# The first four pairs of input tiles of the recurrent stage as seven products, with the residual reloaded behind them

## The chip, the core and the metric

The kernel runs on one core of a Trainium2 chip. The metric is the device time of one execution in microseconds (us); a time is the median of several executions. The trace comes from one execution under the hardware profiler.

## The reference

One decoder layer on 512 tokens of width 1024: a SwiGLU feed-forward, a mixing layer, a second feed-forward, each with an RMS norm in front and behind. The mixing layer, in which the change lies, is

```
u = rms_norm(h, mix_norm_pre)
q, k, v, xr, yr, gl = split(u @ w_in)          # 12 heads of q, k, v; xr, yr: 1024 wide; gl: 2048
attn = dilated_window_attention(q, k, v)        # three groups of heads, joined by their log-sum-exp
xc  = conv4(xr) + conv_b                        # causal, width 4, per channel
gate_x, gate_a = sigmoid(xc_head @ w_x + b_x), sigmoid(xc_head @ w_a + b_a)
log_a = -8 * gate_a * softplus(-a_param);  a = exp(log_a)
rec = scan(a, sqrt(1 - a*a) * gate_x * xc) * gelu(yr)
gates = sigmoid(gl)                             # two of width 1024
merged = gates[0] * (attn @ w_attn) + gates[1] * (rec @ w_rec)
h = h + rms_norm(merged @ w_out, mix_norm_post)
```

## The kernel before, in words

**Precision.** Every float32 operand is split in two float32r parts, hi and lo, by a copy on ACT and a subtraction on DVE (`split`, lines 284 and 285). A product is three matmuls: hi by hi, hi by lo, lo by hi (`mm3`, lines 297 to 299).

**Plain products.** The 512 tokens lie along the free axis. A tile of 128 output columns is `gemm`: 8 blocks of the 1024 inputs by three matmuls of 512 tokens, 24 in all, into one PSUM bank (`acc`, five of them; `aux`, three).

**Seven products.** Most of the feed-forwards and the q, k and first gate columns go another way. Two output tiles (called g and u) by two halves of the tokens by two halves of the input are a 2 x 2 by 2 x 2 block product, done with seven products in place of eight (Strassen and Winograd). Each of the seven is 4 blocks by three matmuls of 256 tokens, 12 matmuls (`seventh`, lines 616 to 618), so a pair of tiles takes 84 matmuls of 256 tokens in place of 48 of 512. It needs forms of both operands: sums of their quarters, split again. The forms of the mixing layer's input `u` are made once, in the attention stage (`forms_of`): p1, p2, p3 are its own quarters in `um`'s tiles, p5 and p7 are in two tiles of the pool tagged "b" (named `big`), p6 and p4 in two slots `tx` of the attention pool. The forms of a pair's weights are made for each pair (`w_forms`): four additions of 128x512 and splits of 1024, 1024, 1024 and 512 columns, in three of the four `w8` slots and one of the two `w4` slots; they need a scratch `s12`. The seven products are put together either by `seven` (three copies out of PSUM by ACT and four sums by DVE) or by `seven_on` (used in the feed-forwards), where the later products are added in PSUM onto copies of the earlier ones: four copies by ACT (one bank to another, or to SBUF), and PE comes back to the copied bank one product later. `seven_on` holds four `acc` banks.

**Order in the mixing layer.** Values; four heads, each with the q and k pairs of the next; four pairs of gate tiles; the attention branch's output product (8 tiles, 96 matmuls); then the recurrent stage in the order of `LRU_ORDER`: conv 0, branch 0, branch 1, conv 1, gates 0, branch 2, conv 2, gates 1, gate1 1, and so on. `conv` makes two tiles of `xr` with a plain product each, copies them in time order (line 1269, a strided copy), runs the four taps on ACT and DVE (1270, 1272) and splits the result into `rec`. `branch` makes two tiles of `yr`, copies them out (1286); `gelus` applies the Gelu for two heads after branches 1 and 3 (1292). `gates` makes the two gates of a head from `rec` (1322), and `recur` does the recurrence (1333 to 1351), and overwrites `rec` with its output.

**Order of the engines.** The program is written in one order, and a planner gives each engine a fixed order of its own by rank. The rank is the place in the program, moved forward by `tc.high_priority(offset)`: weights are fetched and split at `state["ahead"]`, 100 in most of the kernel (AHEAD) and 300 in the recurrent stage (EVAC + AHEAD); emptying a PSUM bank has 200 (EVAC). `w_forms` has 100. An engine then works strictly in its order.

**DMAs.** Weights come in 1 MB pieces through SP's queue into two `raw` buffers, in the order of `stream_plan`. The residual `h` was stored to DRAM as `kept_m` and is reloaded through POOL's queue (four DMAs of 512 KB, line 1216) after the last gate pair, into two tiles of the pool "b", which has six: four hold `um`. It is read again in the boundary behind the out product (line 461).

Of the kernel before, what the change touches and what calls it, by code (L numbers as in the profile page):

```python
# [16 lines left out]
P = 128  # L17
T = 512
# [27 lines left out]

# [37 lines left out]
def part_blocks(a):  # L84

    return (FF_PARTS[a][1] - FF_PARTS[a][0]) // 2


def stream_plan():

    plan = []

    def down(n, a, half):
        for kk in range(part_blocks(a)):
            plan.append((("down", n, a, half, kk), 1024))

    def ffn(n):
        for ev in ffn_order(n):
            if ev[0] == "std":
                plan.append((("gate", n, ev[1]), 1024))  # L100
                plan.append((("up", n, ev[1]), 1024))
            elif ev[0] == "prep":
                plan.append((("gu", n, ev[1]), 2048))
            elif ev[0] == "down":
                down(n, *ev[1:])
            elif ev[0] == "prepd":
                for q in SEVEN_RAW[ev[2]]:
                    plan.append((("dq", n, ev[1], q), 1024))
        for half in range(2):
            down(n, len(FF_PARTS) - 1, half)  # L110

    def values(g):
        for k in range(4):
# [12 lines left out]
    for h in range(NH):  # L126
        qk(h)
    for c in range(0, KC, 2):
        plan.append((("pair", 52 + c, 53 + c), 2048))
    for m in range(KC):  # L130
        plan.append((("attn", m), 512))
    for what, h in LRU_ORDER:
        if what == "gates":
            plan.append((("lru", h), 1024))
        else:
            cs = GATE1[h] if what == "gate1" else (2 * h, 2 * h + 1)
            o = {"conv": 36, "branch": 44, "gate1": 60}[what]
            for c in cs:
                plan.append((("in", o + c), 1024))
    for m in range(KC):  # L140
        plan.append((("rec", m), 1024))
    for half in range(2):
        for kk in range(4):
            plan.append((("out", half, kk), 1024))
    ffn(2)
    return plan
# [25 lines left out]
def hybrid_layer(ctx: ExitStack, tc: tile.TileContext, xT: bass.AP, xN: bass.AP, wst: bass.AP,  # L172
# [365 lines left out]
    def tx_slot(pool, bufs=1):  # L538
        return pool.tile([P, 2, 4, HB], F32R, name="tx", tag="tx", bufs=bufs)

    def forms_of(x, his, los, pool, copied):


        spool[0] = pool
        fx = facc.rearrange("p k t -> p (k t)").rearrange("p (b c) -> p b c", b=4)

        def quarter(i, j):
            return fx[:, 2 * j:2 * j + 2, i * T:i * T + T]

        def slot():  # L550
            return tx_slot(pool, 1 if copied else 2).rearrange("p s k t -> p s (k t)").rearrange(
                "p s (b c) -> p s b c", b=2)
# [36 lines left out]
    spool = [None]  # L589

    def w_forms(key):

        with tc.high_priority(offset=AHEAD):
            raw = raw_of(key)
            u0, u1, g0, g1 = (raw[:, i * 512:(i + 1) * 512] for i in range(4))
            s12 = spool[0].tile([P, 2, 512], F32, name="s12", tag="s", bufs=2)
            DVE.tensor_add(s12[:, 1, :], u0, u1)  # L597
            DVE.tensor_add(s12[:, 0, :], s12[:, 1, :], g0)
            DVE.tensor_add(u0, u0, g0)
# [17 lines left out]
            PE.matmul(ps, wh, xl, start=False, stop=False, skip_group_check=True)  # L617
            PE.matmul(ps, wl, xh, start=False, stop=k == 3, skip_group_check=True)  # L618

    def seven_on(t, w, g, u):  # L620

        b, z, y, v = (acc_ps()[:, :HB] for _ in range(4))
        lo, hi = HALVES

        def copy(ps, dst=None):
            if dst is None:
# [2 lines left out]
                ACT.activation(dst, ps, AF.Copy)  # L631
            return dst

        def sum_of(dst, ps, c):
            with tc.high_priority(offset=EVAC):
                DVE.tensor_add(dst, ps, c)

        seventh(t, w, "p1", b, True)
        copy(b, y)
        seventh(t, w, "p5", z, True)  # L640
# [1 line left out]
        seventh(t, w, "p6", b, False)  # L642
        c6 = copy(b)
        seventh(t, w, "p2", y, False)
        ACT.activation(g[:, lo], y, AF.Silu)
        seventh(t, w, "p7", b, False)
        copy(b, v)
        sum_of(u[:, hi], b, c5)
        seventh(t, w, "p3", z, False)
        sum_of(g[:, hi], z, c6)  # L650
        ACT.activation(g[:, hi], g[:, hi], AF.Silu)
        seventh(t, w, "p4", v, False)
        return v

    def seven(t, w, z, g, u, seen=lambda ap: ap):

# [32 lines left out]
    def ffn(n, x, r, forms_x, apool, pss):  # L689
# [101 lines left out]
        def prod(f, w):  # L791
            g, u = tmp("g"), tmp("u")
            if f >= FIRST_ON[n]:
                v = seven_on(t, w, g, u)

                def put(dst, view):
                    for q, (h, src) in enumerate(zip(HALVES, (v, u[:, HALVES[1]]))):
                        DVE.scalar_tensor_tensor(dst[:, q] if len(dst.shape) == 3 else dst[:, h], g[:, h], -1.0, src,
                                                 op0=ALU.mult, op1=ALU.mult)
                into(f, put)  # L800
# [192 lines left out]
    ff1.close()  # L993


    with ExitStack() as mx:
        tpl = mx.enter_context(tc.tile_pool(name="attn_out", bufs=1))
        apool_cm = tc.tile_pool(name="attention", bufs=1)
# [51 lines left out]
        t, steps = forms_of(um, um_t[:2], um_t[2:], apool, False)  # L1050
        values(VALUES[0], True)
        attn_t = tpl.tile([P, 8, T], F32R, name="attn", tag="attn")
        attn = Act([attn_t[:, i, :] for i in range(4)], [attn_t[:, 4 + i, :] for i in range(4)])
# [157 lines left out]
            ACT.activation(facc[:, c, :], g, AF.Sigmoid)  # L1211
            ACT.activation(facc[:, c + 1, :], u, AF.Sigmoid, scale=-1.0)
        apool_cm.__exit__(None, None, None)
        new_h()
        for b in range(4):
            nc.gpsimd.dma_start(hb(b), kept_m[b])
        for c in range(KC):
            ps = acc_ps()
            gemm(ps, fetch(("attn", c)), attn)
# [1 line left out]

    with ExitStack() as mx:
        rpool = mx.enter_context(tc.tile_pool(name="rec", bufs=1))
        rec_t = rpool.tile([P, 16, T], F32R, name="rec")
        rec = Act([rec_t[:, i, :] for i in range(8)], [rec_t[:, 8 + i, :] for i in range(8)])
        sig = rpool.tile([P, KC, T], F32, name="sig")
        lpool_cm = tc.tile_pool(name="lru", bufs=1)
        lpool = lpool_cm.__enter__()

# [27 lines left out]
        def pi(ap):  # L1257
            return ap.rearrange("q (p i) -> q p i", p=4)

        def conv(hd):  # L1260

            for c in (2 * hd, 2 * hd + 1):
                ps = acc_ps()
                gemm(ps, fetch(("in", 36 + c)), um)
                xr = lpool.tile([P, 3 + T], F32, name="xr", tag="xr", bufs=2)
                DVE.memset(xr[:, 0:3], 0.0)
                xc = sig[:, c, :]
                with tc.high_priority(offset=EVAC):
                    DVE.tensor_copy(ip(xr[:, 3:]), pi(ps))
                    ACT.activation(xc, xr[:, 3:], AF.Identity, bias=col("cb", c), scale=col("cw", 3 * 8 + c))  # L1270
                    for t in (2, 1, 0):
                        DVE.scalar_tensor_tensor(xc, xr[:, t:t + T], col("cw", t * 8 + c), xc,
                                                 op0=ALU.mult, op1=ALU.add)
                    split(rec.hi[c], rec.lo[c], xc)
# [3 lines left out]
        def branch(hd):  # L1278

            gels[hd] = []  # L1280
            for c in (2 * hd, 2 * hd + 1):
                ps = acc_ps()
                gemm(ps, fetch(("in", 44 + c)), um)
# [67 lines left out]
                DVE.tensor_mul(pi(ge), ip(th), pi(ge))  # L1351
                split(rec.hi[c], rec.lo[c], ge)

        state["ahead"] = EVAC + AHEAD
        for what, hd in LRU_ORDER:
            if what == "gates":
                recur(hd, gels.pop(hd), *gates_of(hd))
            else:
# [13 lines left out]
        for c in range(KC):  # L1372
# [5 lines left out]
            DVE.tensor_mul(sig[:, c, :], ps, sig[:, c, :])  # L1378
            DVE.tensor_add(sig[:, c, :], sig[:, c, :], facc[:, c, :])
            split(mg.hi[c], mg.lo[c], sig[:, c, :])  # L1380


    ap2 = ctx.enter_context(tc.tile_pool(name="act2", bufs=1))
# [141 lines left out]
```

## Time and profile before

| | |
|---|---|
| median of 3 runs | 1227.24 us (1226.72 to 1227.56) |
| the profiled execution | 1227.1 us |
| its span in the trace | 1225.3 us |
| granted TensorE clock | 0.999 |
| the four pairs conv 0, branch 0, branch 1, conv 1 | 636.74 to 680.26 us of the span |
| the recurrent stage to the last gate | to about 800 us |

PE is TensorE's matmuls, PEld its weight loads, DVE VectorE, ACT ScalarE, POOL GpSimd, SP the queue that issues the weight DMAs. A row of a timeline has the start, the duration, engine, line, operation, output and inputs, and in brackets the idle time before it. The end of a matmul is modelled and overlaps the next, so its price is the distance between starts. A row of a group has the count, the busy time, the mean duration in ns, the idle time before and what ended it. The residual's reload stands at 611 to 614 us.

### The profile page before, as it was taken

What the parts mean: (1) busy time and instruction counts of PE and PEld (TensorE: products, weight loads), DVE (VectorE), ACT (ScalarE), POOL (GpSimd) and SP (SyncE); (2) the same over time, 40 slices, a digit from 0 to 9 for tenths busy, and PEclk for the clock granted to TensorE, in tenths of its full rate; (3) what the DMA queues carried; (4) which work ended last, traced back from release to release, by engine and by line L of the source; (5) the groups of instructions that cost most, each with busy time, mean ns of one, the idle gap of its engine ahead of it and who ended that gap; (6) DMA issues with size and microseconds to landing.
All of it is one profiled execution on the core that took longest, in us unless ns stands there. A gap on an engine that the chain in (4) does not pass through costs nothing.

```text
span 1225.3 us, 19182 instructions
## 1 busy us (share of the span) xinstructions
PE 1214.1 (99%) x7700; PEld 1102.8 (90%) x7700; DVE 981.5 (80%) x1497; ACT 784.0 (64%) x1337; POOL 26.1 (2%) x51
## 2 busy tenths in 40 slices
PE   9999999999999999999999999999999999999997
PEld 8899999999878899999988888888899999999996
DVE  7988888899677587888565897785798888889975
ACT  7556777777555365665543888844566677878752
POOL 0000000000002000000000000000100000000000
PEclk9999999999999999999999999999999999999999
DMA  6223333334614222222252222234453333333341
GB/s 246 89 84 121 121 121 121 121 121 167 245 69 146 89 93 103 79 78 103 73 204 74 98 104 74 98 110 168 151 156 121 121 120 121 121 120 121 138 172 69
DMA packets 29401, 148.73 MB, mean 121 GB/s; under 512 B 3200, under 2 KB 6400, under 8 KB 15232
## 3 DMA queue, kind: packets, MB, share of 16 engines
q1 hardware_dynamic: 22032, 130.20, 29.4%
q0 software_dynamic: 7280, 17.30, 4.1%
q8 instruction: 60, 0.98, 0.3%
q14 instruction: 29, 0.24, 0.1%
HBM read 137.01 MB, written 6.29 MB: 117 GB/s over the span
## 4 chain that ended last, share of the span: by engine, by line
PE 93%; DVE 3%; ACT 2%; DMA 1%; issue 0%; DVEq 0%; ACTq 0%
PE acc L616 14%; PE acc L617 14%; PE acc L618 14%; PE acc L297 8%; PE acc L298 8%; PE acc L299 8%; PE aux L879 3%; PE aux L880 3%; PE aux L881 3%; PE acc L403 2%; PE acc L405 2%; PE acc L404 2%; PE acc L1025 1%; PE acc L1027 1%; PE acc L1026 1%; DMA raw<-in_w 1%
## 5 line engine op out<-in xcount | busy, mean ns | idle before, releaser
L285 DVE TENSOR_TENSOR w<-raw,w 128x1024 fp32r<-128x1024 f32 (+1 forms) x274 | 296.3, 1086 | 75.8 <-ACT w L284 68.8
L616 PE MATMUL acc<-big,w 128*128 128x256 f32 x1208 | 342.8, 284 | 0.4 <-ACT c L631 0.4
L617 PE MATMUL acc<-big,w 128*128 128x256 f32 x1208 | 342.7, 284 | 0.0
L618 PE MATMUL acc<-big,w 128*128 128x256 f32 x1208 | 342.4, 283 | 0.0
L284 ACT ACTIVATE w<-raw 128x1024 fp32r<-128x1024 f32 (+1 forms) x274 | 258.5, 949 | 120.1 <-PE acc L299 36.7
L616 PEld LDWEIGHTS acc<-big,w 128*128 128x128 f32 x1208 | 231.5, 192 | 2.4 <-ACT c L631 1.0
L617 PEld LDWEIGHTS acc<-big,w 128*128 128x128 f32 x1208 | 231.6, 192 | 1.4
L618 PEld LDWEIGHTS acc<-big,w 128*128 128x128 f32 x1208 | 231.6, 192 | 0.0
L616 PE MATMUL acc<-tx,w 128*128 128x256 f32 x276 | 78.5, 284 | 0.0
L617 PE MATMUL acc<-tx,w 128*128 128x256 f32 x276 | 78.1, 283 | 0.0
L618 PE MATMUL acc<-tx,w 128*128 128x256 f32 x276 | 78.1, 283 | 0.0
L879 PE MATMUL aux<-w,xf 128*128 128x512 f32 x196 | 76.4, 393 | 0.8 <-ACT w L284 0.8
L880 PE MATMUL aux<-w,xf 128*128 128x512 f32 x196 | 76.6, 391 | 0.0
L881 PE MATMUL aux<-w,xf 128*128 128x512 f32 x196 | 76.3, 389 | 0.0
L297 PE MATMUL acc<-big,w 128*128 128x512 f32 x192 | 74.7, 389 | 0.0
L298 PE MATMUL acc<-big,w 128*128 128x512 f32 x192 | 74.7, 389 | 0.0
L299 PE MATMUL acc<-big,w 128*128 128x512 f32 x192 | 74.7, 389 | 0.0
L284 ACT ACTIVATE w<-s 128x1024 fp32r<-128x1024 f32 x53 | 56.0, 1058 | 19.7 <-PE acc L618 13.9
L285 DVE TENSOR_TENSOR w<-s,w 128x1024 fp32r<-128x1024 f32 x53 | 64.6, 1218 | 4.2 <-ACT w L284 4.2
L597 DVE TENSOR_TENSOR s<-raw 128x512 f32<-128x512 f32 x53 | 36.4, 687 | 32.7 <-DMA raw<-in_w 32.7
L616 PEld LDWEIGHTS acc<-tx,w 128*128 128x128 f32 x276 | 52.9, 192 | 0.1
L617 PEld LDWEIGHTS acc<-tx,w 128*128 128x128 f32 x276 | 52.9, 192 | 0.0
(367 smaller groups left out, 2572.2 us busy)
## 6 DMA issues: line engine op xcount, KB each, us to landing
raw<-in_w SPq DMA_DIRECT2D x110, 1024.0 KB, 4.8
raw<-in_w SPq DMA_DIRECT2D x14, 512.0 KB, 3.6
big<-xf POOLq DMA_DIRECT2D x6, 512.0 KB, 3.2
gains<-in_rows POOLq DMA_DIRECT2D x5, 512.0 KB, 4.9
h<-in_x SPq DMA_DIRECT2D x8, 256.0 KB, 5.1
h<-in_xn POOLq DMA_DIRECT2D x4, 512.0 KB, 5.6
kept_m<-h POOLq DMA_DIRECT2D x4, 512.0 KB, 2.9
h<-kept_m POOLq DMA_DIRECT2D x4, 512.0 KB, 5.2
```

The lines of the kernel that those rows point to most:

```text
L284: ACT.activation(dh, src, AF.Copy)
L285: DVE.tensor_sub(dl, src, dh.bitcast(F32))
L297: PE.matmul(ps, wh, xh, start=first, stop=False)
L298: PE.matmul(ps, wh, xl, start=False, stop=False)
L299: PE.matmul(ps, wl, xh, start=False, stop=last)
L597: DVE.tensor_add(s12[:, 1, :], u0, u1)
L616: PE.matmul(ps, wh, xh, start=start and k == 0, stop=False, skip_group_check=True)
L617: PE.matmul(ps, wh, xl, start=False, stop=False, skip_group_check=True)
L618: PE.matmul(ps, wl, xh, start=False, stop=k == 3, skip_group_check=True)
L879: PE.matmul(ps, xh, wh, start=first and j == 0, stop=False, skip_group_check=True)
L880: PE.matmul(ps, xh, wl, start=False, stop=False, skip_group_check=True)
L881: PE.matmul(ps, xl, wh, start=False, stop=j == 1, skip_group_check=True)
```

## The change

The first four input pairs of `LRU_ORDER` (conv 0, branch 0, branch 1, conv 1) are made with `seven_on` from the forms of the input that the attention stage made. The weights are streamed in pairs (the same bytes, in the same 1 MB pieces). `seven_on` takes functions for the four places where a half tile is finished; in the feed-forwards they do what they did, here they are four half-width DVE instructions at 200. The forms of the first pair are prepared in front of the stage at 100, those of the next at the start of each pair at 300, with `s12` in a free part of `sig`. The forms p6 and p4 now lie in one tile `rb` of a pool `keep` that stays open to the end of the stage; the second half of `rec` takes the same tile once the four pairs are done. The residual is reloaded there too, since p5 and p7 hold its two tiles until then.

```diff
+PAIRED = LRU_ORDER[:4]
+COLUMN = {"conv": 36, "branch": 44, "gate1": 60}
...
+        elif (what, h) in PAIRED:
+            plan.append((pair_key(what, h), 2048))
...
         def slot():
-            return tx_slot(pool, 1 if copied else 2).rearrange(
+            if not copied and not two:
+                v = rb()
+                two.extend(v[:, 4 * i:4 * i + 4, :].rearrange("p (s j) t -> p s j t", s=2) for i in range(2))
+            if two:
+                return two.pop(0)
+            return tx_slot(pool).rearrange("p s k t -> p s (k t)").rearrange("p s (b c) -> p s b c", b=2)
...
-    def w_forms(key):
+    def w_forms(key, s12=None):
-        with tc.high_priority(offset=AHEAD):
+        with tc.high_priority(offset=state["ahead"]):
...
-            s12 = spool[0].tile([P, 2, 512], F32, name="s12", tag="s", bufs=2)
+            if s12 is None:
+                s12 = spool[0].tile([P, 2, 512], F32, name="s12", tag="s", bufs=2)
...
-    def seven_on(t, w, g, u):
+    def seven_on(t, w, g0, g1, u0, u1):
...
         seventh(t, w, "p2", y, False)
-        ACT.activation(g[:, lo], y, AF.Silu)
+        g0(y)
         seventh(t, w, "p7", b, False)
         copy(b, v)
-        sum_of(u[:, hi], b, c5)
+        u1(b, c5)
         seventh(t, w, "p3", z, False)
-        sum_of(g[:, hi], z, c6)
-        ACT.activation(g[:, hi], g[:, hi], AF.Silu)
+        g1(z, c6)
         seventh(t, w, "p4", v, False)
-        return v
+        u0(v)
...
+    kpool_cm = tc.tile_pool(name="keep", bufs=1)
+    kpool = kpool_cm.__enter__()
+
+    def rec_half():
+        return kpool.tile([P, 8, T], F32R, name="rb", tag="rb")
...
         apool_cm.__exit__(None, None, None)
-        new_h()
-        for b in range(4):
-            nc.gpsimd.dma_start(hb(b), kept_m[b])
...
+        def prepare(i):
+            paired[PAIRED[i]] = w_forms(pair_key(*PAIRED[i]), sig[:, 4 + i % 2 * 2:6 + i % 2 * 2, :])
+
+        def pair_next(key):
+            if PAIRED.index(key) + 1 < len(PAIRED):
+                prepare(PAIRED.index(key) + 1)
+            return paired.pop(key)
+
+        prepare(0)
+        state["ahead"] = EVAC + AHEAD
...
+        def pairs_to(w, g, u, view, half):
+            def up(dst, ps, sign):
+                with tc.high_priority(offset=EVAC):
+                    if sign > 0:
+                        DVE.tensor_copy(half(dst, 0), view(ps))
+                    else:
+                        DVE.tensor_scalar(half(dst, 0), view(ps), -1.0, None, op0=ALU.mult)
+            def low(dst, ps, c, sign):
+                with tc.high_priority(offset=EVAC):
+                    if sign > 0:
+                        DVE.tensor_add(half(dst, 1), view(ps), view(c))
+                    else:
+                        DVE.scalar_tensor_tensor(half(dst, 1), view(ps), -1.0, view(c), op0=ALU.mult, op1=ALU.subtract)
+            seven_on(t, w, lambda y: up(g, y, 1), lambda z, c: low(g, z, c, 1), lambda v: up(u, v, -1),
+                     lambda b, c: low(u, b, c, -1))
...
         def conv(hd):
...
+            if ("conv", hd) in PAIRED:
+                w = pair_next(("conv", hd))
+                pairs_to(w, *(xr_of(2 * hd + i) for i in range(2)), lambda ap: ap.rearrange("q (p i) -> q p i", p=2),
+                         lambda x, i: x[:, 2 * i:2 * i + 2, :])
...
         def branch(hd):
...
+            if ("branch", hd) in PAIRED:
+                w = pair_next(("branch", hd))
+                gels[hd] = [lpool.tile([P, T], F32, name="ge", tag="ge", bufs=6) for _ in range(2)]
+                pairs_to(w, *gels[hd], lambda ap: ap, lambda x, i: x[:, HALVES[i]])
+                return
...
         for what, hd in LRU_ORDER:
+            if len(paired) == 0 and rec.hi[4:] == [] and (what, hd) not in PAIRED:
+                rec_t = rec_half()
+                rec.hi += [rec_t[:, i, :] for i in range(4)]
+                rec.lo += [rec_t[:, 4 + i, :] for i in range(4)]
+                new_h()
+                for b in range(4):
+                    nc.gpsimd.dma_start(hb(b), kept_m[b])
```

More of the change, by code (lines that the diff above doesn't have):

```diff
@@ L86, in part_blocks, with pair_key @@
     return (FF_PARTS[a][1] - FF_PARTS[a][0]) // 2
+def pair_key(what, h):
+    c = COLUMN[what] + 2 * h
+    return "pair", c, c + 1
 def stream_plan():
@@ L134, in stream_plan @@
             plan.append((("lru", h), 1024))
-        else:
[L136 to L139, printed above, removed]
+        elif (what, h) in PAIRED:
+            plan.append((pair_key(what, h), 2048))
+        else:
+            for c in GATE1[h] if what == "gate1" else (2 * h, 2 * h + 1):
+                plan.append((("in", COLUMN[what] + c), 1024))
     for m in range(KC):
@@ L539, in tx_slot, with forms_of @@
         return pool.tile([P, 2, 4, HB], F32R, name="tx", tag="tx", bufs=bufs)
-    def forms_of(x, his, los, pool, copied):
+    def forms_of(x, his, los, pool, copied, rb=None):
         spool[0] = pool
@@ L548, in quarter @@
             return fx[:, 2 * j:2 * j + 2, i * T:i * T + T]
+        two = []
         def slot():
-            return tx_slot(pool, 1 if copied else 2).rearrange("p s k t -> p s (k t)").rearrange(
-                "p s (b c) -> p s b c", b=2)
+            if not copied and not two:
[4 more added lines that the diff above has]
+            return tx_slot(pool).rearrange("p s k t -> p s (k t)").rearrange("p s (b c) -> p s b c", b=2)
         x01, x10, x11 = quarter(0, 1), quarter(1, 0), quarter(1, 1)
@@ L618, in seventh @@
             PE.matmul(ps, wl, xh, start=False, stop=k == 3, skip_group_check=True)
-    def seven_on(t, w, g, u):
+    def seven_on(t, w, g0, g1, u0, u1):
         b, z, y, v = (acc_ps()[:, :HB] for _ in range(4))
-        lo, hi = HALVES
         def copy(ps, dst=None):
@@ L632, in copy @@
             return dst
-        def sum_of(dst, ps, c):
-            with tc.high_priority(offset=EVAC):
-                DVE.tensor_add(dst, ps, c)
         seventh(t, w, "p1", b, True)
@@ L793, in prod, with g1, u1, u0 @@
             if f >= FIRST_ON[n]:
[L794 to L800, printed above, removed]
+                lo, hi = HALVES
+                def g1(z, c6):
+                    with tc.high_priority(offset=EVAC):
+                        DVE.tensor_add(g[:, hi], z, c6)
+                    ACT.activation(g[:, hi], g[:, hi], AF.Silu)
+                def u1(b, c5):
+                    with tc.high_priority(offset=EVAC):
+                        DVE.tensor_add(u[:, hi], b, c5)
+                def u0(v):
+                    def put(dst, view):
+                        for q, (h, src) in enumerate(zip(HALVES, (v, u[:, hi]))):
+                            DVE.scalar_tensor_tensor(dst[:, q] if len(dst.shape) == 3 else dst[:, h], g[:, h], -1.0,
+                                                     src, op0=ALU.mult, op1=ALU.mult)
+                    into(f, put)
+                seven_on(t, w, lambda y: ACT.activation(g[:, lo], y, AF.Silu), g1, u0, u1)
                 return
@@ L1048, in values @@
                 vals[g] = nv
-        t, steps = forms_of(um, um_t[:2], um_t[2:], apool, False)
+        t, steps = forms_of(um, um_t[:2], um_t[2:], apool, False, rec_half)
         values(VALUES[0], True)
@@ L1223, in hybrid_layer @@
         rpool = mx.enter_context(tc.tile_pool(name="rec", bufs=1))
-        rec_t = rpool.tile([P, 16, T], F32R, name="rec")
-        rec = Act([rec_t[:, i, :] for i in range(8)], [rec_t[:, 8 + i, :] for i in range(8)])
+        rec_t = rpool.tile([P, 8, T], F32R, name="rec")
+        rec = Act([rec_t[:, i, :] for i in range(4)], [rec_t[:, 4 + i, :] for i in range(4)])
+        rec.n = KC
         sig = rpool.tile([P, KC, T], F32, name="sig")
+        paired = {}
+        def prepare(i):
[6 more added lines that the diff above has]
+        state["ahead"] = EVAC + AHEAD
         lpool_cm = tc.tile_pool(name="lru", bufs=1)
@@ L1258, in pi, with xr_of @@
             return ap.rearrange("q (p i) -> q p i", p=4)
-        def conv(hd):
-            for c in (2 * hd, 2 * hd + 1):
[L1263 to L1267, printed above, removed]
+        def pairs_to(w, g, u, view, half):
+            def up(dst, ps, sign):
+                with tc.high_priority(offset=EVAC):
+                    if sign > 0:
[3 more added lines that the diff above has]
+            def low(dst, ps, c, sign):
+                with tc.high_priority(offset=EVAC):
+                    if sign > 0:
[4 more added lines that the diff above has]
+                     lambda b, c: low(u, b, c, -1))
+        def conv(hd):
+            xrs = {}
+            def xr_of(c):
+                xrs[c] = lpool.tile([P, 3 + T], F32, name="xr", tag="xr", bufs=2)
+                DVE.memset(xrs[c][:, 0:3], 0.0)
+                return ip(xrs[c][:, 3:])
+            if ("conv", hd) in PAIRED:
+                w = pair_next(("conv", hd))
+                pairs_to(w, *(xr_of(2 * hd + i) for i in range(2)), lambda ap: ap.rearrange("q (p i) -> q p i", p=2),
+                         lambda x, i: x[:, 2 * i:2 * i + 2, :])
+            for c in (2 * hd, 2 * hd + 1):
+                if c not in xrs:
+                    ps = acc_ps()
+                    gemm(ps, fetch(("in", 36 + c)), um)
+                    with tc.high_priority(offset=EVAC):
+                        DVE.tensor_copy(xr_of(c), pi(ps))
+                xr, xc = xrs[c], sig[:, c, :]
                 with tc.high_priority(offset=EVAC):
-                    DVE.tensor_copy(ip(xr[:, 3:]), pi(ps))
                     ACT.activation(xc, xr[:, 3:], AF.Identity, bias=col("cb", c), scale=col("cw", 3 * 8 + c))
@@ L1352, in recur @@
                 split(rec.hi[c], rec.lo[c], ge)
-        state["ahead"] = EVAC + AHEAD
         for what, hd in LRU_ORDER:
+            if len(paired) == 0 and rec.hi[4:] == [] and (what, hd) not in PAIRED:
[5 more added lines that the diff above has]
+                    nc.gpsimd.dma_start(hb(b), kept_m[b])
             if what == "gates":
@@ L1380, in hybrid_layer @@
             split(mg.hi[c], mg.lo[c], sig[:, c, :])
+    kpool_cm.__exit__(None, None, None)
     ap2 = ctx.enter_context(tc.tile_pool(name="act2", bufs=1))
```

## The prediction, made before the result was known

> **What bounds the kernel now.** I read the busy times first, then the chain of work that ended last, then stretches of the stage that changes.
>
> ```profile
> span 1225.3 us, 19182 instructions
> PE 1214.1 (99%) x7700; PEld 1102.8 (90%) x7700; DVE 981.5 (80%) x1497; ACT 784.0 (64%) x1337; POOL 26.1 (2%) x51
> PE 93%; DVE 3%; ACT 2%; DMA 1%; issue 0%; DVEq 0%; ACTq 0%
> ```
>
> PE is busy 99% of the span and makes up 93% of the chain, so time can come only from fewer or shorter matmuls, or be lost by making PE wait. The next view is stretches of the recurrent stage: the first four rows are the four pairs of input products that the change touches (conv 0, branch 0, branch 1, conv 1), the last two the rest of the stage. The columns are the length, then the busy time of PE, PEld, DVE, ACT and POOL with their instructions, the granted clock, the DMA share and GB/s.
>
> ```profile
> 636.74:647.62 10.88, 10.88 (x50) 9.01 (x49) 7.12 (x9) 3.04 (x4) 0.00 (x0) 1.00 0.30 110
> 647.62:658.50 10.88, 10.88 (x50) 9.01 (x49) 7.38 (x10) 5.49 (x6) 0.00 (x0) 1.00 0.26 96
> 658.50:669.38 10.88, 10.88 (x50) 9.01 (x49) 3.84 (x4) 3.16 (x4) 0.00 (x0) 1.00 0.26 98
> 669.38:680.26 10.88, 10.88 (x50) 9.01 (x49) 6.46 (x8) 4.06 (x5) 0.00 (x0) 1.00 0.29 96
> 680.26:720.00 39.74, 39.74 (x177) 32.92 (x176) 35.83 (x49) 33.44 (x45) 0.00 (x0) 1.00 0.22 80
> 720.00:800.00 80.00, 80.00 (x355) 66.24 (x354) 63.47 (x83) 65.72 (x84) 0.00 (x0) 1.00 0.26 92
> ```
>
> PE never rests here, at full clock. DVE does: 7.12 + 7.38 + 3.84 + 6.46 = 24.8 us of 43.5, so 18.7 us are idle; ACT is busy 15.8 us. Behind the four pairs DVE is nearly full (35.83 of 39.74).
>
> Busy times of matmuls overlap, so the price of a matmul is taken from starts in the timeline: the first instruction of one stretch to the first of the next.
>
> ```profile
> 604.87 0.28 PE L616 MATMUL acc<-big,w 128*128 128x256 f32 x1
> ...
> 614.83 0.28 PE L618 MATMUL acc<-big,w 128*128 128x256 f32 x1
> 614.95 0.40 PE L297 MATMUL acc<-attn,w 128*128 128x512 f32 x1
> ```
> ```profile
> 636.74 0.39 PE L297 MATMUL acc<-big,w 128*128 128x512 f32 x1
> ```
> ```profile
> 680.03 0.39 PE L299 MATMUL acc<-big,w 128*128 128x512 f32 x1
> 680.26 0.39 PE L297 MATMUL aux<-rec,w 128*128 128x512 f32 x1
> ```
>
> The last gate pair of the attention stage, seven products of 12 matmuls, runs from 604.87 to 614.95: 84 matmuls in 10.08 us, 120 ns each. The four pairs of plain products run from 636.74 to 680.26: 4 x 48 = 192 matmuls in 43.52 us, 227 ns each, 10.88 us a pair.
>
> **The change part by part.** *Matmuls.* 4 x 48 of 512 columns go, 4 x 84 of 256 columns come: 4 x 10.08 = 40.32 us against 43.52. If PE keeps its pace, **3.2 us** are gained. The operands lie as they did in the attention stage (p1 to p3 in the input's tiles, p5 and p7 in big tiles, p6 and p4 now in one tile of the keep pool in place of two slots), so 120 ns is a measured price, not a guess.
>
> *DVE.* Now the elementwise price, from groups by line and shape (560 to 636 us, then 636.74 to 690).
>
> ```profile
> L285 DVE TENSOR_TENSOR w<-raw,w 128x1024 fp32r<-128x1024 f32 x9 | 10.9, 1223 | 5.8 <-PE acc L618 3.2 <-ACT w L284 2.5
> L285 DVE TENSOR_TENSOR w<-raw,w 128x512 fp32r<-128x512 f32 x11 | 7.5, 684 | 1.1 <-ACT w L284 1.1
> L602 DVE TENSOR_TENSOR raw<-s,raw 128x512 f32<-128x512 f32 x3 | 2.0, 681 | 0.0
> L671 DVE TENSOR_TENSOR u<-acc,c 128x256 f32<-128x256 f32 x4 | 1.7, 421 | 1.1 <-PE acc L618 1.1
> ```
> ```profile
> L1272 DVE SCALAR_TENSOR_TENSOR sig<-xr,first,sig 128x512 f32<-128x512 f32 x12 | 9.0, 747 | 0.3
> L1269 DVE COPY xr<-acc 128x512 f32<-128x512 f32 x4 | 4.3, 1084 | 6.1 <-PE acc L299 6.1
> L285 DVE TENSOR_TENSOR rec<-sig,rec 128x512 fp32r<-128x512 f32 x4 | 2.8, 691 | 1.7 <-ACT rec L284 1.7
> L1286 DVE COPY ge<-acc 128x512 f32<-128x512 f32 x4 | 2.8, 690 | 9.1 <-PE acc L299 9.1
> ```
>
> The weights of a pair cost two splits before (2 x 1.22 = 2.4 us). As forms they cost four additions of 512 columns (4 x 0.68), three splits of 1024 (3 x 1.22) and one of 512 (0.68): 7.1 us. Emptying the banks costs 2 x 0.69 in a branch and 2 x 1.08 in a conv before; afterwards four half-width instructions, 4 x 0.42 = 1.7 in a branch. The strided half of a conv is not in the trace: between 0.42 and 1.08, and I take half of 1.08, 0.54, since the instruction does half the elements of that row; 2.2 a pair. That is 4.6 to 4.9 us more a pair.
>
> The first pair is prepared in front of the stretch. Inside it stand the forms of three pairs (21.2), the splits for gates 0 and branch 2 (3 x 1.22 = 3.7), the emptying (2 x 1.7 + 2 x 2.2 = 7.8), conv 0's chain (6 x 0.75 + 2 x 0.69 = 5.9) and one product of the attention branch (0.7): 39.3 us in 40.3 of PE. It fits as a sum, but not evenly. While branch 0 is on PE, DVE owes conv 0's chain (5.9), a pair's forms (7.1) and five emptyings (0.54 + 4 x 0.42 = 2.2): 15.2 us in 10.1, 5.1 over. What PE needs of it: the next pair takes the fifth acc bank, and wants two more banks after its first product, of 12 x 0.12 = 1.44 us. The earlier of these were done four and three products before that point, so their emptying may be 5.8 and 4.3 us late. If it stands behind everything else, PE waits 5.1 - 4.3 = 0.8 us at the start of branch 1. It may stand so: the emptying ranks 200 places ahead in program order, the forms of the later pairs 300, and conv 0's chain has the same 200 but is written earlier. If it slips into gaps, nothing is lost; I take **0.4 us**, the middle.
>
> That a full DVE as such does not hold PE is shown by a stretch of the first feed-forward, which has the same sevens and the same forms:
>
> ```profile
> 260.00:280.00 20.00, 20.00 (x139) 18.68 (x138) 19.82 (x25) 15.88 (x28) 0.00 (x0) 1.00 0.23 79
> ```
>
> DVE is busy 19.82 of 20 us there, and PE 20.00. But there the emptying ranks ahead of the forms (200 against 100).
>
> *ACT.* Rows of the same two groupings and of the timeline:
>
> ```profile
> L284 ACT ACTIVATE w<-raw 128x1024 fp32r<-128x1024 f32 x10 | 10.4, 1054 | 5.5 <-DMA raw<-in_w 3.5 <-PE acc L618 2.1
> L666 ACT ACTIVATE c<-acc 128x256 f32<-128x256 f32 x19 | 7.2, 382 | 9.9 <-PE acc L618 9.5
> ```
> ```profile
> 653.30 1.06 ACT L284 ACTIVATE w<-raw 128x1024 fp32r<-128x1024 f32 x1
> 654.38 1.28 ACT L1292 ACT_TABLE_LOAD   x1
> 655.68 0.63 ACT L1292 ACTIVATE ge<-ge 128x512 f32<-128x512 f32 x1
> ```
>
> Each pair adds four copies out of a bank (4 x 0.38 = 1.5 us), and PE returns to that bank one product, 1.44 us, later. So a copy may start 1.44 - 0.38 = 1.06 us late for free: just the length of one form copy. All ACT work in the stretch comes to some 27 us of 40, so few copies meet one, and each that does costs between 0 and 0.2 us (the 0.2 being the longest hop from engine to engine that I allow). I take **0.2 us** in all. A table load and a Gelu in front of a copy would cost 1.28 + 0.63 + 0.38 - 1.44 = 0.85 us; that is a rival below.
>
> *Moves that I cost at nothing.* The reload of the residual goes from the attention's end to behind conv 1:
>
> ```profile
> 611.09 1.12 POOL L1216 DMA_DIRECT2D h<-kept_m  x2 [232.69 <-PE acc L618]
> 613.08 1.05 POOL L1216 DMA_DIRECT2D h<-kept_m  x2 [0.87 <-ACT c L666]
> 837.06 1.15 POOL L421 DMA_DIRECT2D gains<-in_rows  x2 [222.93 <-DVE big L285]
> ```
> ```profile
> L461 DVE SCALAR_TENSOR_TENSOR h<-facc,stat,h x4: 1284/1285/1286, 863.6 to 886.7; 128x1024 f32<-128x1024 f32 x4
> ```
>
> POOL issues nothing between it and 837, so its wait for the big tiles of p5 and p7 (free after conv 1's fifth product, about 674) holds nobody, and the residual is first read at 863.6. Its 2 MB meet weight loads on queues busy 0.22 of the time. Without that cover one weight load would be late by its share, at most the median 5.2 us of a residual load, less what two raw buffers hold ahead. The second half of the recurrent stage's output waits for p4 of conv 1, and is first written by conv 2, some 25 us on: nothing. The sign changes of the up half ride in instructions that are there anyway.
>
> *Sum.* -3.2 + 0.4 + 0.2 = **-2.6 us**. The profiled execution took 1227.1 us (span 1225.3), which would become 1224.5; against the median of 1227.24 it is **1224.6 us**. What ends last stays PE.
>
> **The rivals.** *DVE late (B).* The emptying stands behind forms at more than one pair. Against the 0.8 us priced at branch 1, it would be 0.8 at each of three boundaries and the first gates too, 3.2 in all: 1227.2 at worst, around 1226.2. For it: the ranks, 300 before 200. Against: outside branch 0 no pair owes more than 10.1.
>
> *ACT late (C).* A table load and Gelu before a copy, 0.85 us once, 1225.3; if all 16 copies were late by 0.2 us as well, 1227.2 or more. For it: the Gelus of branches 0 and 1 fall among the pairs. The Trainium skill, "ScalarE: Activation LUTs", section "What ACT_TABLE_LOAD costs", puts a switch of tables at about 2.66 us, as 1.28 for the load and 1.38 for a drain; by it the wait would be 2.2 us in place of 0.85 and the sum -0.6. The trace agrees on the load alone: the Gelu starts 1.30 us after it.
>
> *Slower (D): DVE's backlog reaches the gates.* The stretch adds 39.3 - 24.8 = 14.5 us of DVE work to 40.3 - 24.8 = 15.5 us of room. If half that room cannot be used, because forms wait for weight slots that only PE sets free, 6.7 us go over into 680 to 720, where DVE has 3.9 us idle, and conv 1's chain, which gates 1 reads, is that late: -3.2 + 6.7 = +3.5, 1230.7 us. It decides from a backlog of 3.2 + 2.45 = 5.65 us on. Against: conv 1's chain has gates 0 and 21.8 us of branch 2 and conv 2 to hide under.
>
> *It doesn't do what it says (E).* The pairs run at 120 ns, but the planner fills the same gaps differently and PE waits elsewhere for as much: 1227.2.
>
> **How the numbers follow.** Forecast, 1224.6 with stalls of 0 to 1.2 us (1224.0 to 1225.2): 0.62. B 0.14, C 0.08, D 0.12, E 0.04. A measurement of this kernel tells about 0.2%, 2.45 us, from no change, so faster means under 1224.8 and slower over 1229.7. Of the forecast 0.50 lies under 1224.8 and 0.12 above; B, C and E are within. Faster 0.50, same 0.12 + 0.14 + 0.08 + 0.04 = 0.38, slower 0.12. The range begins at the full gain less the spread of the runs, 1227.24 - 3.2 - 0.5 = 1223.5, and ends at 1227.4, where B, C and E end; D is left out.
>
> **What would show it.** Right: four stretches of 84 matmuls 10.1 us long from the first product of conv 0 on, gates 0 some 2.6 us earlier, DVE above 8.5 tenths in them, and everything behind shifted by as much. Stalls at the first copies or at the first use of a bank in branch 1 show B or C by the releaser named. Wrong: matmuls in the pairs further apart than 120 ns, or a wait of gates 1 for the split of conv 1 (D).

## The result and the profile after

The changed kernel took 1238.85 us (median of 5 runs, 1237.41 to 1239.96), the kernel before 1227.19 beside it: a ratio of 1.0095, 95% interval 1.008 to 1.0109. It is **slower by 11.7 us** where I had forecast 2.6 us faster; the range ended at 1227.4. The profiled execution is the fastest of the five: 1237.41 us, span 1235.6 against 1225.3. One execution of a later version (first pair at 300) took 1317 us at a granted clock of 0.849; it is left out of that version's time.

The whole loss lies between the end of the attention branch and the first read of the residual in the boundary. Before, the pairs begin at 636.74 us and that read at 863.6, 226.9 us later; after, at 637.05 and 873.9, 236.9 us later. These 10.0 us are the difference of the spans to within 0.3; what follows the stage is unchanged. The first matmul of the pairs and the first read of the residual after the change:

```profile
637.05 0.28 PE L633 MATMUL acc<-big,w 128*128 128x256 f32 x1
```
```profile
L471 DVE SCALAR_TENSOR_TENSOR h<-facc,stat,h x4: 1283/1284/1285, 873.9 to 897.0; 128x1024 f32<-128x1024 f32 x4
```

The same stage in stretches, columns as in the prediction:

```profile
637.05:650.00 12.95, 9.05 (x67) 8.07 (x65) 12.75 (x17) 7.46 (x11) 0.00 (x0) 1.00 0.02 6
650.00:664.00 14.00, 13.95 (x115) 13.72 (x114) 12.23 (x18) 7.39 (x11) 0.00 (x0) 1.00 0.46 161
664.00:670.60 6.60, 0.34 (x4) 0.14 (x2) 6.60 (x13) 2.34 (x5) 0.00 (x0) 0.73 0.33 138
670.60:674.00 3.40, 3.40 (x17) 3.40 (x18) 0.43 (x4) 2.62 (x4) 0.00 (x0) 0.53 0.00 0
674.00:700.00 26.00, 25.95 (x182) 24.20 (x181) 17.05 (x26) 17.05 (x26) 2.16 (x4) 1.00 0.56 203
```

PE is busy for 9.05 of 12.95 us in the first row and for 0.34 of 6.60 us in the third, and these are the two rows in which DVE is full (12.75 and 6.60 us). In the fourth row PE is busy but has a granted clock of 0.53. The waits of PE between 630 and 690 us, by releaser, in us, times and the longest:

```profile
PE acc L633 <- ACT acc L647: 6.7, 2, 6.3
PE acc L635 <- DVE w L295: 2.2, 1, 2.2
PE acc L633 <- ACT c L647: 1.2, 1, 1.2
```

From starts of matmuls, as in the prediction, with 120 ns for 256 columns and 227 for 512, PE loses 13.6 us, standing still or running slow, in the 165 us from the first pair on: 5.2 in short waits up to 650, 6.4 in the long one at 664, 1.3 at the lower clock behind it, the rest in single steps. 13.6 less the 3.2 gained is 10.4, near the 10.0 of the stage.

**The short waits.** The first pair's weights have landed by 627.26 us, where ACT's copy for a first split ends its wait for their DMA. DVE's timeline from there on:

```profile
627.26 1.06 ACT L294 ACTIVATE w<-raw 128x1024 fp32r<-128x1024 f32 x1 [0.26 <-DMA raw<-in_w]
```
```profile
628.35 1.23 DVE L295 TENSOR_TENSOR w<-raw,w 128x1024 fp32r<-128x1024 f32 x1 [0.62 <-ACT w L294]
...
634.53 0.69 DVE L1247 TENSOR_TENSOR facc<-acc,facc 128x512 f32<-128x512 f32 x1 [1.36 <-PE acc L309]
637.25 0.69 DVE L614 TENSOR_TENSOR sig<-raw 128x512 f32<-128x512 f32 x1 [2.03 <-PE acc L309]
637.86 0.68 DVE L1247 TENSOR_TENSOR facc<-acc,facc 128x512 f32<-128x512 f32 x1
638.46 0.68 DVE L614 TENSOR_TENSOR sig<-raw 128x512 f32<-128x512 f32 x1
639.06 1.28 DVE L615 TENSOR_TENSOR sig<-sig,raw 128x512 f32<-128x512 f32 x2
```

One split of the first pair runs at once (628.35). The first form addition, the one that writes the scratch in `sig`, comes at 637.25, after an idle time ended by PE: the last matmul of the attention branch, which had started at 636.8. DVE was idle 2.03 us in front of it and had gaps before. So all but 1.2 us of the 7.1 us of form work fall behind 637, with the forms of the second pair between them (638.46 is its first addition: its raw weights have landed too, and it ranks 300 where the first pair ranks 100).

**The long wait.** The ACT copy that PE waits for, and what DVE does before it:

```profile
670.11 0.37 ACT L647 ACTIVATE acc<-acc 128x256 f32<-128x256 f32 x1 [1.57 <-DVE ge L1306]
```
```profile
662.26 0.68 DVE L614 TENSOR_TENSOR sig<-raw 128x512 f32<-128x512 f32 x1
662.86 0.74 DVE L1343 SCALAR_TENSOR_TENSOR sig<-xr,first,sig 128x512 f32<-128x512 f32 x1
...
667.79 0.68 DVE L295 TENSOR_TENSOR rec<-sig,rec 128x512 fp32r<-128x512 f32 x1
668.39 0.68 DVE L295 TENSOR_TENSOR w<-raw,w 128x512 fp32r<-128x512 f32 x1
669.00 0.68 DVE L295 TENSOR_TENSOR rec<-sig,rec 128x512 fp32r<-128x512 f32 x1
669.60 0.42 DVE L1306 COPY ge<-acc 128x256 f32<-128x256 f32 x1
669.93 0.41 DVE L1315 SCALAR_TENSOR_TENSOR ge<-acc,c 128x256 f32<-128x256 f32 x1
```

Branch 0's banks are emptied from 669.60 on, all four in a row (two are shown), behind the fourth pair's forms (662.26 on) and the last of conv 0's chain. Branch 1's first copy needs one of these banks, and PE, which stopped at 664, needs that copy.

### The profile page after: what moved, and what is told of

It is laid out like the page before. It is cut to its first block, busy times and chain, and to the rows that moved or that the text cites. A ratio compares the mean times of both kernels' runs of the same rounds, so it can differ in the third digit from the quotient of the medians.

```text
span 1235.6 us, 19531 instructions
## 1 busy us (share of the span) xinstructions
PE 1213.5 (98%) x7844; PEld 1108.4 (90%) x7844; DVE 996.7 (81%) x1529; ACT 795.1 (64%) x1361; POOL 26.1 (2%) x51
## 4 chain that ended last, share of the span: by engine, by line
PE 90%; DVE 5%; ACT 3%; DMA 1%; issue 0%; DVEq 0%; ACTq 0%
PE acc L633 14%; PE acc L635 14%; PE acc L634 14%; PE acc L307 6%; PE acc L309 6%; PE acc L308 6%; PE aux L902 3%; PE aux L903 3%; PE aux L904 3%; PE acc L415 2%; PE acc L414 2%; PE acc L413 2%; DVE w L295 2%; DMA raw<-in_w 1%; PE acc L1055 1%; PE acc L1057 1%
## 5 line engine op out<-in xcount | busy, mean ns | idle before, releaser
L633 PE MATMUL acc<-big,w 128*128 128x256 f32 x1288 | 366.4, 285 | 2.8 <-ACT c L647 2.2
L635 PE MATMUL acc<-big,w 128*128 128x256 f32 x1288 | 365.6, 284 | 2.2 <-DVE w L295 2.2
L634 PE MATMUL acc<-big,w 128*128 128x256 f32 x1288 | 365.9, 284 | 0.0
L294 ACT ACTIVATE w<-raw 128x1024 fp32r<-128x1024 f32 (+1 forms) x278 | 261.2, 944 | 108.5 <-PE acc L309 32.8
L633 PEld LDWEIGHTS acc<-big,w 128*128 128x128 f32 x1288 | 247.4, 192 | 5.8 <-ACT c L647 3.2
L635 PEld LDWEIGHTS acc<-big,w 128*128 128x128 f32 x1288 | 247.4, 192 | 2.4 <-DVE w L295 2.4
L634 PEld LDWEIGHTS acc<-big,w 128*128 128x128 f32 x1288 | 247.5, 192 | 1.5
L647 ACT ACTIVATE c<-acc 128x256 f32<-128x256 f32 x78 | 29.7, 381 | 40.3 <-PE acc L635 40.0
L633 PE MATMUL acc<-rb,w 128*128 128x256 f32 x160 | 46.1, 288 | 6.3 <-ACT acc L647 6.3
L307 PE MATMUL acc<-big,w 128*128 128x512 f32 x128 | 49.8, 389 | 0.0
L308 PE MATMUL acc<-big,w 128*128 128x512 f32 x128 | 49.8, 389 | 0.0
L309 PE MATMUL acc<-big,w 128*128 128x512 f32 x128 | 49.8, 389 | 0.0
L677 ACT ACTIVATE c<-acc 128x256 f32<-128x256 f32 x72 | 27.3, 380 | 31.5 <-PE acc L635 30.2
L810 ACT ACTIVATE g<-g 128x256 f32<-128x256 f32 x35 | 14.5, 416 | 50.1 <-DVE g L809 50.1
L309 PE MATMUL acc<-xf,w 128*128 128x512 f32 (+1 forms) x136 | 46.1, 339 | 0.0
```

The lines of the kernel that those rows point to most:

```text
L294: ACT.activation(dh, src, AF.Copy)
L307: PE.matmul(ps, wh, xh, start=first, stop=False)
L308: PE.matmul(ps, wh, xl, start=False, stop=False)
L309: PE.matmul(ps, wl, xh, start=False, stop=last)
L633: PE.matmul(ps, wh, xh, start=start and k == 0, stop=False, skip_group_check=True)
```

## The experiments

Theory 1: the form work of the first pair starts late, because its scratch shares a pool with `rec`, whose half lies where the attention branch's input lay; the late work is behind all the waits. Theory 2: rank is behind them, forms at 300 going ahead of the emptying at 200.

**The scratch in a pool of its own.** `rec`'s first half takes the place of the attention branch's input in that tile's own pool, which stays open. The address of `sig` is the same as in the changed kernel, right behind that tile: the scratch itself never overlapped the attention branch's input, only the pool did.

```diff
-        tpl = mx.enter_context(tc.tile_pool(name="attn_out", bufs=1))
+    tpl_cm = tc.tile_pool(name="attn_out", bufs=1)
+    tpl = tpl_cm.__enter__()
...
-        rec_t = rpool.tile([P, 8, T], F32R, name="rec")
+        rec_t = tpl.tile([P, 8, T], F32R, name="rec", tag="attn")
...
+    tpl_cm.__exit__(None, None, None)
```

> The scratch of the first pair's forms no longer lies in a pool laid over the attention branch's input tile, so these forms need not wait for the last attention product. Theory 1 (late start: 6 us of form work pushed into the pairs causes all the stalls): the first form addition runs near 628 us in place of 637, the short stalls at 638 to 648 us (5.0 us) go, and the long one at 664 us (6.5 us, and 1.3 us of slow clock behind it) goes too, since DVE is no longer behind: 1224 to 1226 us. Theory 2 (rank: the emptying of branch 0's banks stands behind conv 0's chain and the forms of the next pair, whatever the start): the short stalls go, the long one stays at 5 us or more: 1231 to 1234 us.

Measured: 1228.47 us, ratio 1.0011 (1.0002 to 1.002). Some 10 of the 11.7 us are gone with this edit alone. The forms now run under the attention branch:

```profile
627.05 0.69 DVE L614 TENSOR_TENSOR sig<-raw 128x512 f32<-128x512 f32 x1
627.65 1.22 DVE L295 TENSOR_TENSOR w<-raw,w 128x1024 fp32r<-128x1024 f32 x1
628.78 0.69 DVE L615 TENSOR_TENSOR sig<-sig,raw 128x512 f32<-128x512 f32 x1
```

The long wait is gone too, so theory 2 alone falls. But PE still loses 4.7 us, counted from the starts as above, so the 1224 to 1226 of theory 1 was missed as well. The waits by releaser:

```profile
PE acc L633 <- ACT c L647: 2.0, 2, 1.1
PE acc L633 <- DVE ge L1316: 0.9, 1, 0.9
PE aux L307 <- ACT w L294: 0.2, 1, 0.2
```

**Emptying first**, the shared pool kept:

```diff
             def up(dst, ps, sign):
-                with tc.high_priority(offset=EVAC):
+                with tc.high_priority(offset=2 * EVAC):
...
             def low(dst, ps, c, sign):
-                with tc.high_priority(offset=EVAC):
+                with tc.high_priority(offset=2 * EVAC):
```

> The four emptying instructions of a pair rank 400 places ahead in place of 200; the late start stays. Theory 1: DVE is still 6 us behind, the stalls move to another instruction that PE needs, such as the forms, and most of the loss stays: 1234 us or more. Theory 2: the long stall with its slow clock goes (7.8 us), the short ones stay (5.0 us): about 1230 to 1232 us.

Measured: 1234.05 us, ratio 1.0057 (1.0045 to 1.007), at the lower end of theory 1's forecast and above that of theory 2. The long wait and its slow clock are gone and the short ones stay, as theory 2 has it; but a new wait of 1.9 us for a copy on ACT comes at 671 us, so part of the loss moved, as theory 1 has it. In this trace the stage is 4.6 us longer than before the change, and the pairs begin 1.8 us later (638.51), for which no run shows a cause.

```profile
PE acc L633 <- ACT c L647: 3.1, 2, 1.9
PE acc L635 <- DVE w L295: 2.1, 1, 2.1
```

**Both edits.**

> Both edits. Either theory: no stall over 0.3 us in the pairs, and the 3.2 us of shorter products show: 1224.0 to 1225.0 us. If it stays above 1227, neither cause accounts for the loss and a third one, such as the copies on ACT or the moved residual, carries it.

Measured: 1226.98 us, ratio 0.9998 (0.9989 to 1.0006): no difference from the kernel before, and above the forecast of 1224 to 1225. What is left by releaser:

```profile
PE acc L633 <- ACT c L647: 2.1, 3, 0.9
```

Three waits for the third copy of a pair, c6, on ACT: my "ACT late", in waits up to 0.9 us. It is a form copy that holds them:

```profile
641.46 0.63 ACT L294 ACTIVATE w<-raw 128x512 fp32r<-128x512 f32 x1 [1.96 <-DVE raw L619]
642.00 1.04 ACT L294 ACTIVATE w<-sig 128x1024 fp32r<-128x1024 f32 x1
642.94 0.36 ACT L647 ACTIVATE c<-acc 128x256 f32<-128x256 f32 x1
```

ACT stood idle for 1.96 us before the first row, since that form copy waits for DVE. The other two rows stand behind it in ACT's order, the wanted copy last.

**Forms at 100**, the shared pool kept:

```diff
-        with tc.high_priority(offset=state["ahead"]):
+        with tc.high_priority(offset=AHEAD):
             raw = raw_of(key)
             u0, u1, g0, g1 = (raw[:, i * 512:(i + 1) * 512] for i in range(4))
```

> The forms of all pairs rank 100 ahead, as in the feed-forwards, so emptying (200) and conv 0's chain (200) go before them; the late start stays. Theory 2: the emptying of branch 0 no longer waits for forms, but still for conv 0's chain, which has become earlier too: the long stall shrinks to under 1 us, the short ones stay: 1230 to 1232 us. Theory 1: the forms of the second and third pair are late instead, and PE waits for a weight form of DVE for 4 us or more: 1234 us or more.

Measured: 1229.68 us, ratio 1.0016 (1.0007 to 1.0025), just under the forecast of theory 2. PE loses 5.6 us by the starts, in many short pieces, and the early waits shrink as well: the 2.2 us for a weight form in the changed kernel are 0.7 at most here. With one rank for all, the second pair's forms no longer go between those of the first (they begin at 644.17, behind the first pair's last split).

**Both: own pool and forms at 100**, the fourth corner of a square.

> The fourth corner of a square of two edits: the scratch in a pool of its own, and the forms of the pairs at rank 100 as in the feed-forwards. If the two causes are late form work and forms going ahead of what PE needs (copies and emptying), nothing is left: stalls under 0.5 us in all and 1224.0 to 1225.0 us. If the stalls that each edit left over (4 us with the own pool alone, 5 us with rank 100 alone) have one more cause in common, for instance that DVE and ACT have too much work in the stretch, 2 us or more remain: 1226 us or more.

Measured: 1225.25 us, ratio 0.9984 (0.9975 to 0.9992); a little over the forecast. PE loses 1.4 us by the starts, of which one wait of 0.4 us has a releaser. The square, as ratios to the kernel before:

| | scratch in the shared pool | in a pool of its own |
|---|---|---|
| forms at 300 | 1.0095 | 1.0011 |
| forms at 100 | 1.0016 | 0.9984 |

In us (1227 times the difference of the ratios, each known to about 1 us), the own pool alone takes away 10.3, the rank alone 9.7, and both together 13.6. So the two causes are not parts that add up. Rank 300 costs 3.3 us where the scratch has its own pool, the shared pool costs 3.9 us where the forms rank 100, and the other 6.4 us are lost only where both meet.

**Copies on ACT first**, with the own pool, emptying at 400 and forms still at 300:

```diff
-    def seven_on(t, w, g0, g1, u0, u1):
+    def seven_on(t, w, g0, g1, u0, u1, ahead=EVAC):
...
-            with tc.high_priority(offset=EVAC):
+            with tc.high_priority(offset=ahead):
                 ACT.activation(dst, ps, AF.Copy)
...
-                     lambda b, c: low(u, b, c, -1))
+                     lambda b, c: low(u, b, c, -1), 2 * EVAC)
```

> The scratch in a pool of its own, emptying and the copies on ACT at 400, forms still at 300. What was left with the own pool and the emptying at 400 were three waits of PE for the third copy of a pair, 2.1 us by the releasers, behind a form copy on ACT. If rank is their cause they go: 1224.0 to 1225.2 us. If ACT simply has no room, they move to a wait for a weight form: 1226 us or more.

Measured: 1225.51 us, ratio 0.9983 (0.9974 to 0.9992), between the two forecasts. Two of the three waits are gone, one of 0.4 us is left:

```profile
PE acc L633 <- ACT c L647: 0.4, 1, 0.4
```

Against both edits without this one the ratio falls from 0.9998 to 0.9983, 1.8 us; the two intervals just touch, and the trace decides: rank is the cause of those two waits, and ACT has the room.

**The moves alone**: no pairs, with the keep pool, `rec` in two halves and the reload behind the attention branch.

```diff
-PAIRED = LRU_ORDER[:4]
+PAIRED = ()
...
-        prepare(0)
+        if PAIRED:
+            prepare(0)
```

> No pair is made in seven products; the keep pool, the recurrence's output in two halves and the new place of the residual's reload stay (with no pairs it comes right before conv 0). The prediction costed these moves at nothing: within 1 us of the kernel before, 1226.5 to 1228.5. If they carry part of the loss, it shows here: 1229 us or more.

Measured: 1227.59 us, ratio 1.0 (0.9991 to 1.001). PE keeps its pace through the stage (no wait in it). The keep pool and the halves of `rec` cost nothing. Here the reload comes before conv 0 (issued at 611.34, near its old place), so this version says nothing of a reload behind conv 1.

**All ranks**: own pool, forms at 100, emptying and copies at 400.

> The scratch in a pool of its own, forms at 100, emptying and copies at 400: PE's needs ahead of everything. If late forms never hold PE, the same as forms at 100 alone, 1224.0 to 1225.0 us; if ranks that far apart make forms late, PE waits for a form of DVE at a pair's start and it is above 1226 us.

Measured: 1225.0 us, ratio 0.9981 (0.9972 to 0.999): the fastest version, 2.3 us under the kernel before, though its interval overlaps those of the two others near 1225. The reload stands behind the pairs' big tiles here, issued from 672.13 on, so at that place it costs less than the pairs gain. The 40.32 us of four pairs, from their first matmul on:

```profile
636.92:677.24 40.32, 39.86 (x325) 39.10 (x324) 34.45 (x52) 24.96 (x40) 1.36 (x3) 1.00 0.40 142
```

DVE has 34.45 us of work there, and PE is busy 39.86.

**The first pair at 300 too**, the shared pool kept:

```diff
-        prepare(0)
         state["ahead"] = EVAC + AHEAD
+        prepare(0)
```

> The changed kernel with one line moved: the first pair's forms rank 300 like the others (100 before); the scratch stays in the shared pool, so they still start near 637 us. If the second pair's forms hurt because they overtake the first pair's (300 against 100, both ready at 637), the early stalls (5.0 us) drop to about 2 and the total falls by 3 us or more: 1233 to 1236 us. If only the lateness counts, nothing changes: 1238 us or more.

Measured: 1234.2 us (median of four executions), ratio 1.0055 (1.0041 to 1.0068), as the overtaking has it: some 5 us of the loss need the second pair's forms to go before the first's. DVE's order is the meant one here: the second pair's first addition stands behind all the forms of the first pair.

**Branches only**: branch 0 and 1 in seven products, the shared pool and rank 300 kept.

```diff
-PAIRED = LRU_ORDER[:4]
+PAIRED = LRU_ORDER[1:3]
...
-        prepare(0)
...
-            if len(paired) == 0 and rec.hi[4:] == [] and (what, hd) not in PAIRED:
+            if (what, hd) == PAIRED[0]:
+                prepare(0)
+            if LRU_ORDER.index((what, hd)) == 3:
```

> Only branch 0 and branch 1 are made in seven products, conv 0 and conv 1 in plain ones; the shared pool and rank 300 stay, and the first pair's forms now have conv 0's 10.9 us of plain products to be made under. The shorter products are worth 2 x 0.8 = 1.6 us. If the loss came from forms that start at 637 and are needed at once, it is gone: 1225.5 to 1227 us. If rank 300 alone makes the emptying late whatever the start, PE waits at branch 1 for 2 us or more: 1228 us or more.

Measured: 1227.47 us, ratio 1.0 (0.9991 to 1.0009), between the two forecasts. With a plain pair of conv 0 as cover the large loss is gone, but PE loses 1.4 us by the starts, 0.6 of it in a wait for an ACT copy, and that eats the 1.6 us of two shorter pairs. How much of the 1.4 us comes from rank 300 was not tested in this version.

## Why the prediction was wrong

*Where the bound is, and the gain.* Right. PE bounds the stage, 84 matmuls take 120 ns each in it, and where PE does not wait the 3.2 us show: in the version with copies first the stage is 2.5 us shorter in the trace (224.3 us from the first pair to the residual's read, against 226.9), with 1.1 us lost by PE.

*"The first pair is prepared in front of the stretch."* **This step failed.** It was read from the place in the program and from when the weights land. Only one split of the eight instructions ran there; the other seven, 5.9 of 7.1 us, ran behind 637.25, because the scratch was allotted in a pool over the attention branch's input. The prediction asked what hides the forms and what they need (weights, slots), but not when the memory of the scratch comes free. The own pool, with `sig` at the same address, showed it: it takes away 10.3 us with the later forms at 300, and 3.9 with all forms at 100. The remark that outside branch 0 no pair owes DVE more than 10.1 us fell with it: conv 0 had 5.9 us more on it.

*The ledger of DVE.* 39.3 us in 40.3 were close as work: in the best version the single durations sum to 38.1, and DVE is busy 34.5, as the sum counts the overlaps of neighbours (about 0.09 us each) twice. It was right that the sum is not what decides, and right that the peak lies under branch 0 (647.00 to 657.10 us in the best version, DVE busy 10.06 of 10.10). **Its price is the second step that failed**: 0.8 us at most, 0.4 taken, against 6.4 of wait and 1.3 of slow clock, which are gone where the emptying ranks first. Two things were left out: the late 5.9 us on top of the 5.1 over, and that the emptying stands as a block behind the fourth pair's forms too, since rank is kept even when PE already waits. The remark that forms rank ahead of the emptying here and not in the feed-forward was made, and then priced as a middle between nothing and 0.8. The rank costs 3.3 us even with an early start (the right column of the square).

*Copies on ACT, 0.2 us.* Too small: 1.2 us of waits for such copies in the changed kernel, 2.1 us with both edits. The price for a form copy in front was that of its own length, 1.06; the form copy itself waited for DVE, and ACT with it.

*A rank I had in the text and did not use.* The first pair's forms at 100 and the later ones at 300 meet when both are ready, which the late start brought about: about 5 us.

*Moves at nothing.* Right for the pools and `rec` in two halves: 1.0 (0.9991 to 1.001). The reload behind conv 1 was not run by itself; the version with all ranks has it there and is faster than the kernel before.

*Rivals.* "DVE late" was the right mechanism, priced at 3.2 us at worst where all that PE lost came to 13.6; with ACT's 0.2 kept in, its worst was 1227.4, not 1227.2. "ACT late" is a part of it. "Slower" had the wrong place: no backlog reached gates 1; PE was held inside the pairs. Its 14.5 us of added work also set a sum of durations (39.3) against a busy time (24.8), which counts overlaps once. No rival held the late start, and the chance of slower, 0.12, was too small for a stretch whose ledger left DVE 1 us of 40.

## What to carry to other kernels

When work is moved in front of a stretch, ask for each of its instructions what memory it writes and who last used any part of that pool, not only whether its input is there; in this kernel a scratch in a pool laid over a live tile was a wait, though the scratch did not overlap the tile. When an engine is near full, a sum that fits says little: write down the order in which its queue will stand at the peak, and price a wait by everything ranked ahead, not by the excess of the sum. What PE waits for next (copies and emptied banks) should rank ahead of what it needs a pair later.

## What the runs showed of the hardware

A wait of 6.26 us cost more than itself. PE's timeline in the changed kernel:

```profile
663.99 0.28 PE L635 MATMUL acc<-big,w 128*128 128x256 f32 x1
670.53 0.58 PE L633 MATMUL acc<-rb,w 128*128 128x256 f32 x1 [6.26 <-ACT acc L647]
670.91 0.41 PE L633 MATMUL acc<-big,w 128*128 128x256 f32 x1
671.12 0.41 PE L634 MATMUL acc<-big,w 128*128 128x256 f32 x1
...
673.88 0.28 PE L633 MATMUL acc<-rb,w 128*128 128x256 f32 x1
673.99 0.28 PE L634 MATMUL acc<-rb,w 128*128 128x256 f32 x1
```

Behind it matmuls start 213 ns apart, not 120, until 673.88: 1.3 us are lost in these steps. The granted clock is the number behind the busy times:

```profile
663.99:667.00 3.01, 0.28 (x3) 0.07 (x1) 3.01 (x5) 0.36 (x1) 0.00 (x0) 1.00 0.72 302
667.00:673.80 6.80, 3.27 (x15) 3.27 (x16) 4.03 (x11) 4.40 (x8) 0.00 (x0) 0.50 0.00 0
673.85:680.00 6.15, 6.10 (x51) 5.90 (x50) 3.26 (x5) 3.01 (x5) 0.00 (x0) 1.00 0.00 0
```

The clock falls 3.0 us after the last matmul has started, and is back 3.3 us after the next one. After the wait of 2.16 us at 643.79 there is one slow step of 0.22 us and no drop of the clock. The Trainium skill, "TensorE: Matmul & The Clock Gate", section "What's actually happening", says that the clock halves after an idle window of about 3.4 us and comes back after as long a busy one. This trace comes near it: no drop in 2.16 us of idle time, a drop after 3.0, and a return after 3.3 us of slow matmuls.
